# Two value chunks side by side at the start of a two-layer decoder trunk

## The chip, the cores and the metric

The kernel runs on one core of one Trainium2 chip. The metric is the device time of one execution in microseconds, the median of several runs. Beside the runs there is one profiled execution with its trace; times in it are counted from its first instruction.

## The reference

A decoder trunk of two layers over 256 positions of width 2048, in float32. Layer 1 is a block-sparse self-attention with 16 heads of 128 (with 256 positions there is a single block, so it is plain causal attention with a relative bias), layer 2 a sliding-window attention with shared keys and values. Each is followed by an output projection, a LayerNorm, a convolutional gated feed-forward part of width 5504 and a second LayerNorm. What the change touches is the start of layer 1:

```python
q, k, v = jnp.split(x @ w_qkv, 3, axis=-1)      # (256, 2048) @ (2048, 6144)
...
p = jax.nn.softmax(logits + bias)               # per head
out = p @ v
```

## The kernel before

All weights lie in one stream in memory, `wst`, cut into units of 128 x 1024 float32 (512 KB), in the order in which they are used. A unit is loaded into `raw` by SP (L103, four buffers). It is then split into a high part `wh` by ScalarE (L128) and a low remainder `wl` by VectorE (L157), with four buffers for these. TensorE multiplies high by high, high by low and low by high. The same split is made of x: `xc` is loaded (L220), ScalarE makes the high half of `xT` (L224), VectorE the low half (L225).

The order of work is written out by hand. `take()` hands out the next unit to TensorE; before that it queues the splits up to three units ahead (`AHEAD`), and after them whatever was left for this place with `at(n, ...)`, where n counts steps. `step()` is called after each unit and runs what was left with `pe_at`. So on ScalarE and VectorE, work that `at` left stands behind the split of the unit three ahead. The split of unit u needs the buffers of unit u - 4, which TensorE must have finished.

Layer 1 treats the 16 heads in four groups. `v_group()` computes 512 columns of the value projection (a chunk): x is stationary, weights move, and two accumulators of 128 x 512 take the two halves of the positions. A unit of weights holds two blocks of K (128 rows each) of one chunk, so a chunk is 8 units. `evac` copies the accumulators into `vt` (L751, ScalarE, placed with `at(0, ...)`). Then come, for each of the four heads, a query and a key unit pair (`feat_unit`, `ws_unit`: weights stationary, L300 and L303, two units each) and the steps of `attention`. The accumulators `acc` come from a pool of four, the tiles `at` from another of four.

The opening is written out in `load_input`: the first unit is loaded and split in two pieces of 512 columns, with one block of x behind each; then x (two blocks at a time) and units alternate. Between them `tables()` loads the small tables for the bias; a matmul (L275) after the fourth unit makes the bias rows. On POOL, `spread_bias` (L284, `ud` to `band`) and `load_bias` (L288, `band` to `bias`) run for each group of heads; each bias load waits for its band. `load_residual` (L246) loads x a second time, as the residual.

Of the kernel before, what the change touches and what calls it, by code (L numbers as in the profile page):

```python
# [18 lines left out]
P = 128  # L19
T = 256  # L20
D = 2048
KB = D // P
# [15 lines left out]
RAW_BUFS = 4  # L38
HALF_BUFS = 4
AHEAD = HALF_BUFS - 1  # L40
HW = 1024
# [36 lines left out]
def trunk(ctx: ExitStack, tc: tile.TileContext, wst, xT_in, x_in, relb, onehot, umask, sinks, conv_in, ln_g, ln_b, out):  # L78
# [14 lines left out]
    reach, placed = {}, {}  # L93

    def pieces(u):
        return (slice(0, HW // 2), slice(HW // 2, HW)) if u == 0 else (slice(0, HW),)

    def load_weights(behind=None):
        u = todo["load"]
        if u < n_halves:  # L100
            raws[u] = wpool.tile([P, HW], F32, name="raw")
            for j, c in enumerate(pieces(u)):
                nc.sync.dma_start(raws[u][:, c], wst[u][:, c])  # L103
                if behind:
                    behind(j)
            todo["load"] += 1
# [43 lines left out]
    def quad_low(s):  # L150
        q, (wh, wl) = quad[s], placed[s]
        minus(q.bl, q.shape(raws[s][:, 512:]), q.bh.bitcast(F32))
        minus(wl, q.tm[:, 0:HW], wh.bitcast(F32))

    def low_piece(s, c):
        wh, wl = placed[s]
        nc.vector.tensor_tensor(out=wl[:, c], in0=raws[s][:, c], in1=wh[:, c].bitcast(F32), op=ALU.subtract)  # L157

    def split_upto(i, behind=None):
        while todo["low"] <= min(i, n_halves - 1):  # L160
            s = todo["low"]
            high_upto(s, behind)
            if s in quad:
                quad_low(s)
                raws.pop(s - 1)
                load_weights()
            elif len(pieces(s)) == 1:
                if s - 1 in quad:
                    q = quad[s - 1]
                    nc.scalar.activation(q.uh, q.tm[:, 512:], AF.Copy)  # L170
                low_piece(s, slice(0, HW))
                if s - 1 in quad:
                    minus(q.ul, q.tm[:, 512:], q.uh.bitcast(F32))
            placed.pop(s)
            todo["low"] += 1
            if s + 1 not in quad:
                raws.pop(s)
                load_weights()
# [4 lines left out]
    def at(n, f, *a, first=False):  # L183

        fs = before.setdefault(slot["now"] + n, [])
        fs.insert(0 if first else len(fs), (f, a))
# [25 lines left out]
    xT = big.tile([P, KB, 2 * T], F32R, name="xT")  # L212
# [3 lines left out]
    def load_input(pool, tables):  # L216
        xc = pool.tile([P, KB, T], F32, name="xc", bufs=1)

        def load_x(k, n=2):
            (nc.scalar if n == 1 else nc.sync).dma_start(xc[:, k:k + n], xT_in[:, k:k + n, :])  # L220

        def split_x(k, n=2):
            ks = slice(k, k + n)
            nc.scalar.activation(xT[:, ks, 0:T], xc[:, ks], AF.Copy)  # L224
            nc.vector.tensor_tensor(out=xT[:, ks, T:2 * T], in0=xc[:, ks], in1=xT[:, ks, 0:T].bitcast(F32),  # L225
                                    op=ALU.subtract)

        load_weights(lambda j: load_x(j, 1))
        for c in range(1, RAW_BUFS):
            load_x(2 * c)  # L230
            load_weights()
        tables()
        load_x(2 * RAW_BUFS)
        split_upto(0, lambda j: split_x(j, 1))
        for c in range(1, KB // 2):
            if c + RAW_BUFS < KB // 2:
                load_x(2 * (c + RAW_BUFS))
            if c < HALF_BUFS:
                split_x(2 * c)
                split_upto(c)  # L240
            else:
                at(c - HALF_BUFS, split_x, 2 * c)

    def load_residual():
        for t in range(2):
# [145 lines left out]
    def acc_tile():  # L391
        return psum.tile([P, 512], F32, name="acc")
# [310 lines left out]
    def layer_attention(l, rest, stage, turnover):  # L703
        oT = st
        kept = []
        if l:
            norm, turned = rest
            turn, low = turned
            n0 = nexth["i"]
            c = COLS[1]  # L710
            norm(c[0])
            norm(c[1])
            split_upto(n0 + 7)
            norm(c[2])

            def early(t, i):
                if t == 0 and i == 5:
                    pts = [turn(c[j]) for j in range(2)]
                    low(c[0], pts[0])
                    norm(c[3])  # L720
                    low(c[1], pts[1])
                if t == 0 and i == 7:
                    low(c[2], turn(c[2]))
                if t == 1 and i == 1:
                    low(c[3], turn(c[3]))
                if t == 1 and i < HALF_BUFS:
                    split_upto(n0 + 8 + i)

            kept = [acc_tile(), acc_tile()]
            Moving(lambda k: xT[:, k, :], KB).chunk(kept, early=early)  # L730
        pool = stage(f"att{l}")
        bias = pool.tile([P, NH, 2 * P], F32, name="bias", bufs=1)
        if l == 0:
            load_input(pool, lambda: bias_table(pool))
        else:
            nc.vector.tensor_scalar(nsk, sk, -1.0, None, op0=ALU.mult)
        for i, h in enumerate(range(0, NH, 4)):
            n = (4 + 8 * i, 4 * i)[l]
            if l == 0:
                at(n, spread_bias, l, h, h + 4)  # L740
            at(n, load_bias, bias, l, h, h + 4)

        def v_group(accs=None):
            if not accs:
                accs = [acc_tile(), acc_tile()]
                Moving(lambda k: xT[:, k, :], KB).chunk(accs)
            vt = pool.tile([P, 2, 512], F32, name="vt", bufs=1 if l else 2)

            def evac():
                for t in range(2):  # L750
                    nc.scalar.activation(vt[:, t, :], accs[t], AF.Copy)  # L751

            at(0, evac)
            return vt

        def feat_unit(name, bufs):
            acc = acc_tile()
            ws_unit(acc)
            o = pool.tile([P, T], F32, name=name, bufs=bufs)

            def evac():
                nc.scalar.activation(o, acc[:, T:2 * T], AF.Copy)
                nc.vector.tensor_tensor(out=o, in0=acc[:, 0:T], in1=o, op=ALU.add)

            at(0, evac, first=True)
            return o

        if l == 0:
            for g in range(NH // 4):
                vt = v_group()  # L770
                for j in range(4):
                    h = 4 * g + j
                    q = feat_unit("qT", 4)
                    k = feat_unit("kT", 4)
                    attention(pool, l, h, q, vt[:, :, j * P:(j + 1) * P], k, bias, oT)
        else:
            vt = v_group(kept)
            ks = [feat_unit("kT", KVH) for _ in range(KVH)]
            for h in range(NH):
                q = feat_unit("qT", 4)  # L780
                j = h // GRP
                attention(pool, l, h, q, vt[:, :, j * P:(j + 1) * P], ks[j], bias, oT)
        return project_out(lambda k: oT[:, k, :], NH, 2 * l, turnover.homes, AF.Gelu_apprx_tanh, turnover)
# [130 lines left out]
def _moving(w):  # L914

    k, n = w.shape
    b = w.reshape(k // P, P, n // 512, 512).transpose(2, 0, 1, 3).reshape(-1, 2, P, 512)
    return b.transpose(0, 2, 1, 3).reshape(-1, P, HW)


def _paired(w):

    b = w.reshape(FT, P, NCH // 2, 2, 512).transpose(2, 0, 3, 1, 4)
    seq = np.stack([b[n, k, c] for n in range(NCH // 2) for k, c in paired_order(LEAD[n], GROUPS[n])[0]])
    return seq.reshape(-1, 2, P, 512).transpose(0, 2, 1, 3).reshape(-1, P, HW)


def _stream(w_qkv, w_o0, w_kv, w_q, w_o1, w_up, w_down):
    parts = []
    q, k, v = (w_qkv[:, i * D:(i + 1) * D] for i in range(3))  # L930
    for g in range(4):
        c = slice(512 * g, 512 * (g + 1))
        parts.append(_moving(v[:, c]))
        parts.append(np.stack([_still(q[:, c]), _still(k[:, c])], 1).reshape(-1, P, HW))

    def ffn(l):
        up = w_up[l]
        parts.append(np.stack([_still(up[:, :DFF]), _still(up[:, DFF:])], 1).reshape(-1, P, HW))
        parts.append(_paired(w_down[l]))

    parts.append(_moving(w_o0))
    ffn(0)
    parts.append(_moving(w_kv[:, 512:]))
    parts.append(_still(w_kv[:, :512]).reshape(-1, P, HW))
    parts.append(_still(w_q).reshape(-1, P, HW))
    parts.append(_moving(w_o1))
    ffn(1)
    return np.concatenate(parts, 0)
# [36 lines left out]
```

## Time and profile before

| | |
|---|---|
| median of 3 runs | 2074.72 us (2074.56 to 2074.79) |
| profiled execution, its own time | 2074.71 us |
| its span, first to last instruction | 2072.7 us |
| mean granted TensorE clock | 0.998 |
| TensorE, VectorE, ScalarE busy | 99%, 76%, 50% |
| memory read | 401.02 MB |

In a timeline row stand the start, the duration, the engine, the line, the operation with its output and inputs, and the idle time of the engine ahead of it with what ended it. PE is TensorE, DVE VectorE, ACT ScalarE, POOL GpSimd. Matmuls overlap: their durations are longer than the distance from one start to the next, so lost time on TensorE is read from starts. In a row of waits stand the total, the number and the longest. In a row of groups stand the total and the mean (in ns) of one.

### The profile page before, as it was taken

How to read it: one execution, taken by the hardware profiler on the slowest of the kernel's cores; microseconds unless marked ns; L12 is line 12 of the kernel's file. 1: busy time of each engine (PE TensorE's matmuls, PEld its weight loads, DVE VectorE, ACT ScalarE, POOL GpSimd, SP SyncE). 2: the span in 40 equal slices, each digit the busy share in tenths (PEclk: the TensorE clock that was granted, in tenths of full speed). 3: DMA queues.
4: the chain of work that ended last, by engine and by line, in shares of the span. 5: the costliest groups of instructions: out<-in, count | busy, mean ns of one | idle time of the engine just before them, and what ended most of it. 6: DMA issues, size and time to landing. Idle time of an engine off the chain costs nothing.

```text
span 2072.7 us, 28857 instructions
## 1 busy us (share of the span) xinstructions
PE 2058.5 (99%) x11004; PEld 1779.1 (86%) x11004; DVE 1575.2 (76%) x2310; ACT 1031.2 (50%) x1453; POOL 23.3 (1%) x36
## 2 busy tenths in 40 slices
PE   9999999999999999999999999999999999999997
PEld 7888888988888888888888888898888888888886
DVE  5555556787877877898986676788787787788886
ACT  5444444444545555454553555445545454555452
POOL 0100000000000000000000000000000000000000
PEclk9999999999999999999999999999999999999999
DMA  8855558455555555566685545736555555566563
GB/s 282 294 190 180 166 169 274 138 186 192 190 187 191 186 192 185 188 239 202 203 260 193 176 144 169 239 114 197 190 191 184 193 187 189 188 217 214 192 215 131
DMA packets 114266, 405.10 MB, mean 195 GB/s; under 512 B 15648, under 2 KB 15968, under 8 KB 112848
## 3 DMA queue, kind: packets, MB, share of 16 engines
q1 hardware_dynamic: 106832, 383.67, 56.4%
q0 software_dynamic: 7008, 19.33, 2.6%
q8 instruction: 86, 1.41, 0.3%
q14 instruction: 52, 0.43, 0.1%
q10 hardware_dynamic: 288, 0.26, 0.0%
HBM read 401.02 MB, written 6.34 MB: 197 GB/s over the span
## 4 chain that ended last, share of the span: by engine, by line
PE 99%; DVE 0%; DMA 0%; ACT 0%; SPq 0%; issue 0%
PE acc L300 38%; PE acc L303 20%; PE acc L483 6%; PE acc L484 6%; PE acc L485 6%; PE acc L353 5%; PE acc L354 5%; PE acc L355 5%; PE acc L318 1%; PE at L483 1%; PE at L484 1%; PE at L485 1%; PE acc L330 1%; PE at L653 1%; PE at L686 1%; PE at L679 1%
## 5 line engine op out<-in xcount | busy, mean ns | idle before, releaser
L157 DVE TENSOR_TENSOR wl<-raw,wh 128x1024 fp32r<-128x1024 f32 (+1 forms) x639 | 778.4, 1221 | 402.0 <-ACT wh L128 393.4
L128 ACT ACTIVATE wh<-raw 128x1024 fp32r<-128x1024 f32 (+1 forms) x639 | 674.8, 1058 | 685.4 <-issue 249.1
L300 PE MATMUL acc<-xT,wh 128*128 128x512 f32 x3456 | 872.3, 394 | 0.0
L300 PEld LDWEIGHTS acc<-xT,wh 128*128 128x128 f32 x3456 | 623.6, 189 | 112.9
L303 PEld LDWEIGHTS acc<-xT,wl 128*128 128x128 f32 x3456 | 471.4, 190 | 33.8
L303 PE MATMUL acc<-xT,wl 128*128 128x256 f32 x3456 | 481.8, 282 | 0.0
L484 PE MATMUL acc<-wl,up 128*128 128x512 f32 x360 | 140.1, 389 | 0.0
L483 PE MATMUL acc<-wh,up 128*128 128x512 f32 x360 | 140.1, 389 | 0.0
L485 PE MATMUL acc<-wh,up 128*128 128x512 f32 x360 | 140.1, 389 | 0.0
L839 DVE SCALAR_TENSOR_TENSOR work<-work,cw 128x255 f32<-128x255 f32 x172 | 83.2, 484 | 6.1
L840 DVE SCALAR_TENSOR_TENSOR work<-work,cw 128x254 f32<-128x254 f32 x172 | 83.1, 483 | 6.1
L485 PEld LDWEIGHTS acc<-wh,up 128*128 128x128 f32 x360 | 67.6, 188 | 14.1
L483 PEld LDWEIGHTS acc<-wh,up 128*128 128x128 f32 x360 | 67.6, 188 | 14.0
L484 PEld LDWEIGHTS acc<-wl,up 128*128 128x128 f32 x360 | 67.6, 188 | 13.9
L838 DVE TENSOR_SCALAR work<-work,cw 128x256 f32<-128x256 f32 x172 | 70.9, 412 | 6.2
L837 DVE TENSOR_TENSOR work<-acc,work 128x256 f32<-128x256 f32 x172 | 71.7, 417 | 1.5 <-ACT work L836 1.5
L836 ACT ACTIVATE work<-acc 128x256 f32<-128x256 f32 x172 | 62.8, 365 | 6.5 <-PE acc L330 6.5
L353 PE MATMUL acc<-wh,xT 128*128 128x512 f32 x144 | 58.7, 407 | 0.3 <-ACT wh L128 0.3
L354 PE MATMUL acc<-wl,xT 128*128 128x512 f32 x144 | 56.7, 393 | 0.8 <-DVE wl L157 0.8
L355 PE MATMUL acc<-wh,xT 128*128 128x512 f32 x144 | 56.5, 392 | 0.0
L195 ACT ACTIVATE work<-work 128x256 f32<-128x256 f32 x86 | 36.1, 420 | 38.6 <-DVE work L840 38.5
L147 ACT ACTIVATE wh<-work 128x1024 fp32r<-128x1024 f32 x24 | 25.5, 1063 | 47.0 <-DVE work L136 47.0
(197 smaller groups left out, 2210.0 us busy)
## 6 DMA issues: line engine op xcount, KB each, us to landing
raw<-in_wst_dram SPq DMA_DIRECT2D x723, 512.0 KB, 3.4
band<-ud POOLq DMA_DIRECT2D x8, 512.0 KB, 14.6
bias<-band POOLq DMA_DIRECT2D x8, 512.0 KB, 7.3
gb<-in_ln_g_dram POOLq DMA_DIRECT2D x4, 1024.0 KB, 6.3
gb<-in_ln_b_dram POOLq DMA_DIRECT2D x4, 1024.0 KB, 8.1
res<-in_x_dram POOLq DMA_DIRECT2D x2, 1024.0 KB, 7.5
out_dram<-res SPq DMA_DIRECT2D x8, 256.0 KB, 2.5
xc<-in_xT_dram SPq DMA_DIRECT2D x7, 256.0 KB, 5.7
```

What stands on the lines that cost most here:

```text
L128: nc.scalar.activation(wh[:, c], raws[s][:, c], AF.Copy)
L157: nc.vector.tensor_tensor(out=wl[:, c], in0=raws[s][:, c], in1=wh[:, c].bitcast(F32), op=ALU.subtract)
L300: nc.tensor.matmul(acc, cols(wh, j), xT[:, k, :], start=(k == 0), stop=False)
L303: nc.tensor.matmul(o, cols(wl, j), xT[:, k, 0:T], start=False, stop=(k == KB - 1))
L353: nc.tensor.matmul(acc, sh, wh, start=(k == 0), stop=False)
L354: nc.tensor.matmul(acc, sh, wl, start=False, stop=False)
L355: nc.tensor.matmul(acc, sl, wh, start=False, stop=(k == self.nk - 1))
L483: nc.tensor.matmul(acc, a[0], wh, start=key not in begun, stop=False)
L484: nc.tensor.matmul(acc, a[0], wl, start=False, stop=False)
L485: nc.tensor.matmul(acc, a[1], wh, start=False, stop=stop)
L839: nc.vector.scalar_tensor_tensor(c[:, 1:T], h[:, 0:T - 1], w[:, 1:2], c[:, 1:T], op0=ALU.mult, op1=ALU.add)
L840: nc.vector.scalar_tensor_tensor(c[:, 2:T], h[:, 0:T - 2], w[:, 0:1], c[:, 2:T], op0=ALU.mult, op1=ALU.add)
```

## The change

The value projections of the first two groups of heads are computed together, ahead of both groups. A unit of weights now holds one block of K for both chunks (`_moving_two`), the two chunks use four accumulators, and the 16 units run in the order block, chunk, half of the positions (`v_two_groups`). All four copies to `vt` are then placed at once. Chunks 2 and 3 stay as they are. The second unit of weights, like the first, is loaded and split in two pieces. The opening is ordered anew: both units in pieces first, with x in single blocks behind the first unit's pieces, then x, two units, x, the tables, x; the later loads and splits of x are placed by units. The bias loads are placed at other steps.

```diff
     def pieces(u):
-        return (...) if u == 0 else (slice(0, HW),)
+        return (...) if u < 2 else (slice(0, HW),)
...
         load_weights(lambda j: load_x(j, 1))
-        for c in range(1, RAW_BUFS):
-            load_x(2 * c)
-            load_weights()
+        load_weights()
+        load_x(2)
+        load_weights()
+        load_weights()
+        load_x(4)
         tables()
-        load_x(2 * RAW_BUFS)
+        load_x(6)
         split_upto(0, lambda j: split_x(j, 1))
-        for c in range(1, KB // 2):
-            if c + RAW_BUFS < KB // 2:
-                load_x(2 * (c + RAW_BUFS))
-            if c < HALF_BUFS:
-                split_x(2 * c)
-                split_upto(c)
-            else:
-                at(c - HALF_BUFS, split_x, 2 * c)
+        split_upto(1)
+        split_x(2)
+        for k in range(4, KB, 2):
+            if k > 6:
+                at(k - 7, load_x, k)
+            at(k - 3, split_x, k)
...
         for i, h in enumerate(range(0, NH, 4)):
-            n = (4 + 8 * i, 4 * i)[l]
+            n = (10 + 14 * i, 4 * i)[l]
...
+        def v_two_groups():
+            accs = [[acc_tile(), acc_tile()] for c in range(2)]
+            mv = Moving(lambda k: xT[:, k, :], KB)
+            for k in range(KB):
+                for c in range(2):
+                    wh, wl = mv.block()
+                    for t in range(2):
+                        mv.mm(accs[c][t], k, t, wh, wl)
+                step()
+            return [v_evac(a) for a in accs]
...
         if l == 0:
+            vts = v_two_groups()
             for g in range(NH // 4):
-                vt = v_group()
+                vt = vts[g] if g < 2 else v_group()
...
+def _moving_two(w):
+    return w.reshape(-1, P, HW)
...
     for g in range(4):
         c = slice(512 * g, 512 * (g + 1))
-        parts.append(_moving(v[:, c]))
+        if g == 0:
+            parts.append(_moving_two(v[:, 0:1024]))
+        if g > 1:
+            parts.append(_moving(v[:, c]))
```

More of the change, by code (lines that the diff above doesn't have):

```diff
@@ L95, in pieces @@
     def pieces(u):
-        return (slice(0, HW // 2), slice(HW // 2, HW)) if u == 0 else (slice(0, HW),)
+        return (slice(0, HW // 2), slice(HW // 2, HW)) if u < 2 else (slice(0, HW),)
     def load_weights(behind=None):
@@ L746, in v_group, with v_evac @@
                 Moving(lambda k: xT[:, k, :], KB).chunk(accs)
+            return v_evac(accs)
+        def v_two_groups():
[8 more added lines that the diff above has]
+            return [v_evac(a) for a in accs]
+        def v_evac(accs):
             vt = pool.tile([P, 2, 512], F32, name="vt", bufs=1 if l else 2)
```

## The prediction

> **What bounds the kernel now.** I read the page first, then the waits of TensorE, then the opening in order of time, because the diff touches only layer 1's value projection and what is loaded ahead of it. The page's busy times, its chain, and TensorE's waits over the whole span:
>
> ```profile
> span 2072.7 us, 28857 instructions
> ...
> PE 2058.5 (99%) x11004; PEld 1779.1 (86%) x11004; DVE 1575.2 (76%) x2310; ACT 1031.2 (50%) x1453; POOL 23.3 (1%) x36
> ...
> PE 99%; DVE 0%; DMA 0%; ACT 0%; SPq 0%; issue 0%
> ...
> PE at L254 <- POOL ident masks.py:199: 1.4, 1, 1.4
> PE acc L354 <- DVE wl L157: 0.8, 1, 0.8
> PE acc L353 <- ACT wh L128: 0.3, 1, 0.3
> ```
>
> TensorE carries 99% of the chain. It waits three times: for the identity matrix before the warm-up, which the change leaves alone, and twice for the second unit of weights. The diff keeps every matmul (it reorders them and adds none), so it can change the time only by the idle time of TensorE. What there is to win is a part of two waits; everything else it touches can only cost. The waits are listed by modelled matmul ends, so I measure them by starts. TensorE's timeline:
>
> ```profile
> 7.43 0.39 PE L355 MATMUL acc<-wh,xT 128*128 128x512 f32 x1
> ...
> 8.82 0.39 PE L355 MATMUL acc<-wh,xT 128*128 128x512 f32 x1
> 9.49 0.50 PE L353 MATMUL acc<-wh,xT 128*128 128x512 f32 x1 [0.28 <-ACT wh L128]
> 10.75 0.51 PE L354 MATMUL acc<-wl,xT 128*128 128x512 f32 x1 [0.76 <-DVE wl L157]
> 11.09 0.39 PE L355 MATMUL acc<-wh,xT 128*128 128x512 f32 x1
> ...
> 27.70 0.39 PE L355 MATMUL acc<-wh,xT 128*128 128x512 f32 x1
> ...
> 30.42 0.39 PE L355 MATMUL acc<-wh,xT 128*128 128x512 f32 x1
> ```
>
> Between the last two rows lie twelve steps, one unit of weights: 2.72 us, 0.227 us from start to start. After the matmul at 8.82 three more should start at 9.05, 9.28 and 9.50; the third starts at 11.09. So the opening loses 1.59 us, and that is the most the change can win there.
>
> **The opening.** Before, one unit of 512 KB holds two blocks of K for one chunk, so each 2.72 us of matmuls need 512 KB of weights and 256 KB of x. After, a unit holds one block of K for two chunks: 512 KB and 128 KB. The loads are reordered with it, and unit 1 comes in two pieces of 256 KB. ScalarE's timeline shows when the loads land, since each of these rows waited for one:
>
> ```profile
> 5.50 0.63 ACT L128 ACTIVATE wh<-raw 128x512 fp32r<-128x512 f32 x1 [0.38 <-DMA raw<-in_wst_dram]
> ...
> 7.17 0.63 ACT L224 ACTIVATE xT<-xc 128x512 fp32r<-128x512 f32 x1 [0.73 <-DMA xc<-in_xT_dram]
> 8.38 1.06 ACT L128 ACTIVATE wh<-raw 128x1024 fp32r<-128x1024 f32 x1 [0.58 <-DMA raw<-in_wst_dram]
> ...
> 10.32 1.06 ACT L128 ACTIVATE wh<-raw 128x1024 fp32r<-128x1024 f32 x1 [0.36 <-DMA raw<-in_wst_dram]
> ...
> 12.72 1.06 ACT L128 ACTIVATE wh<-raw 128x1024 fp32r<-128x1024 f32 x1 [0.82 <-DMA raw<-in_wst_dram]
> 14.91 1.06 ACT L128 ACTIVATE wh<-raw 128x1024 fp32r<-128x1024 f32 x1 [0.61 <-DMA raw<-in_wst_dram]
> ```
>
> By the order of issue these rows have 768, 1024, 1536, 2304, 3072 and 3840 KB behind them. I read the new order off that curve by its bytes, as estimates: the first piece of unit 1 (1024 KB) at 7.17, the second (1280) halfway to 8.38, at 7.78, x blocks 2 and 3 (1536) at 8.38, unit 2 (2048) at 9.67, unit 3 (2560) at 11.12, unit 4 (3584) at 14.18.
>
> Unit 0's twelve matmuls start as before and end at 9.05: its weights and x blocks 0 and 1 are still issued first. A piece costs one high and one low split:
>
> ```profile
> L157 DVE TENSOR_TENSOR wl<-raw,wh 128x1024 fp32r<-128x1024 f32 x33 | 40.2, 1223 | 31.9 <-ACT wh L128 31.8
> L157 DVE TENSOR_TENSOR wl<-raw,wh 128x512 fp32r<-128x512 f32 x2 | 1.4, 692 | 4.3 <-ACT wh L128 4.3
> L225 DVE TENSOR_TENSOR xT<-xc,xT 128x512 fp32r<-128x512 f32 x7 | 4.8, 687 | 0.6 <-ACT xT L224 0.6
> ```
>
> ScalarE then does unit 1's pieces from 7.17 and 7.80 (0.63 each), x 2 and 3 from 8.43, unit 2 from 9.67 to 10.73. VectorE does the low halves by 8.5 and 9.2, x by 9.84, and unit 2 from 10.76 to 11.99. TensorE asks for unit 1's first piece at 9.05 and 9.28, for its second at 10.41, and for unit 2 at 11.77 (high) and 12.00 (low). All are there, unit 2 with 0.01 us to spare. Unit 3 is asked for at 14.5 and split by 13.4; unit 4 is asked for at about 18.0, behind the bias table's two matmuls, and split by 16.6. The additional instructions (one issue on SP, one split on ScalarE, one on VectorE) lie inside these waits for loads. So the opening wins 1.59 us; as unit 2 has no margin and the curve is read between rows, I allow 0.6 us of new wait: the gain is between 1.0 and 1.6, and I take 1.59. The other x splits and the loads of x move one unit or more later, but a block is now used up in 2.72 us instead of 1.36, and each is still split three units ahead of its use.
>
> **What the change adds: the end of the two chunks.** There are four accumulators of this pool. Before, a chunk holds two, and the first query unit takes a third at once. After, the two chunks hold all four, and the first query unit takes the first again: it cannot start before ScalarE has copied that one out. That copy is put on ScalarE's queue behind the high split of the unit three ahead, and this split waits for the buffers of the very last unit of the chunks. The same order is in the trace at the end of chunk 0, where nothing on TensorE waits for it. Timeline, and the copy by shape:
>
> ```profile
> 30.65 1.98 PE L300 MATMUL acc<-xT,wh 128*128 128x512 f32 x8
> 30.84 1.06 ACT L128 ACTIVATE wh<-raw 128x1024 fp32r<-128x1024 f32 x1 [1.66 <-PE acc L355]
> 31.81 1.06 ACT L751 ACTIVATE vt<-acc 128x512 f32<-128x512 f32 x2
> 31.94 1.22 DVE L157 TENSOR_TENSOR wl<-raw,wh 128x1024 fp32r<-128x1024 f32 x1 [1.50 <-ACT wh L128]
> ...
> L751 ACT ACTIVATE vt<-acc 128x512 f32<-128x512 f32 x2 | 1.1, 582 | 0.0
> ```
>
> The last matmul starts at 30.42, the split at 30.84, the copies at 31.81, the first of them is done 0.58 later, at 32.39. TensorE follows ScalarE by 0.05 us (the split of 8.38 ends at 9.44, its matmul starts at 9.49). So the query matmul that started at 30.65 would start at 32.44: 1.79 us. The first step after such a gap was 0.34 instead of 0.23 (10.75 to 11.09), which adds 0.11: 1.90 us. Bounds: zero if the copy came out ahead of the split, 2.4 if the second copy were waited for too (0.48 more). I take 1.90, since the queue's order in the changed kernel is this one. The first accumulator is complete nine matmuls, 2.04 us, before the chunks' end, so the wait is one of queue order alone. Behind it, the key unit's accumulator is copied 0.48 us after the first and asked for 5 us later; the other two copies and the next split lie within the first query half. Nothing further is late.
>
> **What moves at no cost.** Only one handover from attention to a value chunk goes (chunk 1's own); TensorE waited at none of them, so this is worth nothing. The bias loads are queued on POOL at other places. POOL does not wait for TensorE's place in the program, only for its own transfers, so what counts is the order in its queue: the two residual loads now stand after the first bias load instead of after the third.
>
> ```profile
> 42.30 0.79 POOL L288 DMA_DIRECT2D bias<-band  x1 [13.73 <-DMA band<-ud]
> ...
> 73.09 0.78 POOL L288 DMA_DIRECT2D bias<-band  x1 [15.71 <-DMA band<-ud]
> 73.87 1.10 POOL L246 DMA_DIRECT2D res<-in_x_dram  x2
> 74.92 1.16 POOL L284 DMA_DIRECT2D band<-ud  x1
> ...
> raw<-in_wst_dram SPq DMA_DIRECT2D x723, 512.0 KB, 3.4
> ...
> raw<-in_wst_dram SPq DMA_DIRECT2D x6, 512.0 KB, 7.3
> res<-in_x_dram POOLq DMA_DIRECT2D x2, 1024.0 KB, 7.5
> band<-ud POOLq DMA_DIRECT2D x1, 512.0 KB, 17.7
> ```
>
> (The row with x723 is the page's, the last three are the DMA view of 74 to 92 us; the last column is the time to landing.) So the residual and one band run together at about 43 us instead of 74 us. At 74 us weights then took 7.3 us to land and TensorE never waited. The first bias is needed eight units (21.8 us) later than before and comes no later, so that gets looser. Cost: none, unless the cover is gone, which is the last rival.
>
> **Sum.** 0.31 us are added (1.90 less 1.59). The profiled execution took 2074.71 us, 2.0 more than its span of 2072.7, and the median of the runs is 2074.72, so the same sum holds for both: 2075.0 us. About 0.2%, 4.1 us, is what a measurement of this kernel can tell from no change; this is a thirteenth of it.
>
> **Rivals.** *The opening is not cured.* If unit 2 lands later than the curve says, its low split makes TensorE wait again, by at most the 1.59 that was lost before: 1.90 more, 2076.6 at worst. For it: 0.01 us of margin. Against: less data is ahead of it, and up to 10.32 the curve rises without a break. *The copy comes free.* If TensorE did not wait at the end of the chunks, the gain stays alone: 2073.1. For it: the accumulator is complete 2.04 us early. Against: the order on ScalarE shown above.
>
> *The clock falls back.* The warm-up rows show the clock at work: the first matmul pitch is 0.42 us, and only from the one at 7.43 on it is 0.23.
>
> ```profile
> 1.37 4.10 PE L254 MATMUL at<-ident 128*128 128x128 f32 x18 [1.37 <-POOL ident masks.py:199]
> ...
> 5.77 0.63 PE L354 MATMUL acc<-wl,xT 128*128 128x512 f32 x1
> 6.19 0.63 PE L355 MATMUL acc<-wh,xT 128*128 128x512 f32 x1
> ```
>
> The slow stretch is 6.06 us, from 1.37 to 7.43. If the new gap brought it back, half of such a stretch, 3.0 us, would be added: 2078.0. Against: after the gap of 1.59 us the matmul at 11.09 took 0.39 again. The Trainium skill's page TensorE: Matmul & The Clock Gate, section "A second HAM failure mode: psum-queue depth-cycling", says that short idle times between groups that cycle through accumulators made the clock fall back, which speaks against holding all four; its table in Part 1 asks for an idle window of about 3.4 us. By the first the time would be the 2078.0 of this rival, by the second the 2075.0 above.
>
> *Slower: weights late beside the residual.* From 43 us on, residual and band could hold back the weights. A load goes out when the low split frees its buffer, at 33.16 for the split of 31.94, which is 2.74 after the start of unit 7's last matmul, and is the load of unit 15. Unit 15 is asked for 0.23 + 7 x 2.72 = 19.27 after that start, less 1.2 for its split: the load has 15.4 us. Were it held for the whole of residual and band, 7.5 + 17.7 = 25.2 us, TensorE would wait 9.8 us: 2084.8. It decides from a landing time of 15.4 us, and passes 0.2% from about 19.3. For it: the x loads now reach further into this time. Against: 7.3 in the same company. The Trainium skill's page DMA: Bandwidth & Descriptors, section "Issuing engines are not separate DMA queues", says that transfers of all issuing engines interleave on the same 16; the 7.3 us, beside 3.4 over the whole kernel, agree with sharing, not with standing behind.
>
> **How the numbers follow.** Forecast 0.70 (2074.9 to 2075.6), opening not cured 0.12 (to 2076.6), copy free 0.09 (2073.1), clock 0.04, late weights 0.05. The range 2073.1 to 2076.8 takes in the first three. Only late weights pass 4.1 us upward: slower 0.04, and no case wins 4.1 us: faster 0.02 for what I do not see; same 0.94.
>
> **What would show it.** Right: no gap over 0.5 us in TensorE's starts between 7.4 and 17; one of about 2.0 us from start to start at about 50 us, ahead of the first query unit, put down to ScalarE's copy; matmuls of 0.39 behind it. Wrong: a wait for unit 2's low split near 12 us, no gap at the first query unit, steps of 0.42 after it, or waits for weights between 45 and 75 us. Any change beyond 0.31 that lies behind 60 us would be a cause that I have not named.

## The result and the profile after

| | before | after |
|---|---|---|
| median of 22 runs | 2074.6 us (2074.25 to 2076.39) | 2077.74 us (2075.72 to 2079.73) |
| profiled execution | 2074.71 us | 2078.07 us |
| its span | 2072.7 us | 2076.2 us |

The ratio is 1.0014 (95% interval 1.0008 to 1.002): slower by 3.1 us, beyond the interval and above the forecast range of 2073.1 to 2076.8. It is below the 0.2% named in the prediction, but the trace shows where nearly all of it is. The changed kernel also scatters over 4 us from run to run, where the kernel before mostly stays within 0.5.

TensorE's waits in the changed kernel (total, number, longest, us), and its timeline:

```profile
PE acc L300 <- ACT vt L766: 2.9, 1, 2.9
PE at L254 <- POOL ident masks.py:199: 1.4, 1, 1.4
PE acc L354 <- DVE wl L157: 0.5, 1, 0.5
PE acc L353 <- ACT xT L224: 0.2, 1, 0.2
```

```profile
6.41 0.40 PE L353 MATMUL acc<-wh,xT 128*128 128x512 f32 x1
...
11.21 0.39 PE L353 MATMUL acc<-wh,xT 128*128 128x512 f32 x1
12.14 0.50 PE L354 MATMUL acc<-wl,xT 128*128 128x512 f32 x1 [0.54 <-DVE wl L157]
12.48 0.40 PE L355 MATMUL acc<-wh,xT 128*128 128x512 f32 x1
...
50.87 0.39 PE L355 MATMUL acc<-wh,xT 128*128 128x512 f32 x1
54.20 2.50 PE L300 MATMUL acc<-xT,wh 128*128 128x512 f32 x8 [2.95 <-ACT vt L766]
56.50 1.91 PE L303 MATMUL acc<-xT,wl 128*128 128x256 f32 x8
58.21 0.63 PE L300 MATMUL acc<-xT,wh 128*128 128x512 f32 x1
```

The new gap is there, at the place that was named, but it is 3.33 us from start to start (50.87 to 54.20) instead of about 2.0. Behind it the eight matmuls of 256 columns (L303) span 1.91 us, where they spanned 1.12 in the kernel before:

```profile
32.46 1.12 PE L303 MATMUL acc<-xT,wl 128*128 128x256 f32 x8
```

The granted clock is the share of its full speed that TensorE was given, 1.00 being all of it. In the changed kernel it was (in each row, behind the two ends of a stretch: us, then each engine's busy time and instruction count, then the clock, the DMA share and GB/s):

```profile
50.00:55.00 5.00, 2.05 (x9) 1.39 (x8) 2.12 (x2) 2.39 (x4) 0.00 (x0) 1.00 1.03 380
55.00:59.00 4.00, 4.00 (x16) 3.55 (x15) 0.50 (x1) 1.67 (x3) 0.00 (x0) 0.59 0.73 236
59.00:70.00 11.00, 11.00 (x65) 9.67 (x64) 5.08 (x6) 4.66 (x6) 1.90 (x2) 0.99 0.75 212
...
54.20:55.74 1.54, 1.54 (x7) 1.28 (x8) 0.72 (x1) 1.41 (x3) 0.00 (x0) 1.00 0.81 314
55.74:59.15 3.41, 3.41 (x14) 3.03 (x13) 0.65 (x1) 1.06 (x1) 0.00 (x0) 0.50 0.74 231
```

The clock fell back to half for 3.41 us, from 55.74 to 59.15 (0.59 in the mean from 55 to 59). It did so 1.54 us after the gap had ended: the first seven matmuls behind the gap still ran at full clock. What made the gap longer stands in ScalarE's timeline:

```profile
48.57 1.06 ACT L128 ACTIVATE wh<-raw 128x1024 fp32r<-128x1024 f32 x1 [1.66 <-PE acc L355]
52.61 1.06 ACT L128 ACTIVATE wh<-raw 128x1024 fp32r<-128x1024 f32 x1 [2.97 <-DMA raw<-in_wst_dram]
53.57 2.04 ACT L766 ACTIVATE vt<-acc 128x512 f32<-128x512 f32 x4
```

The split of unit 19 waited for its weights, not for its buffer. By the prediction's own offsets it would have started at 51.29 (0.42 behind the matmul at 50.87); it started at 52.61, 1.32 us later, and the copy behind it was as late. POOL's timeline, and the DMA view of 42 to 56 us (the last column is the time to landing):

```profile
40.76 1.10 POOL L246 DMA_DIRECT2D res<-in_x_dram  x2
41.81 1.15 POOL L284 DMA_DIRECT2D band<-ud  x1
63.59 0.79 POOL L288 DMA_DIRECT2D bias<-band  x1 [20.63 <-DMA band<-ud]
...
raw<-in_wst_dram SPq DMA_DIRECT2D x5, 512.0 KB, 9.3
band<-ud POOLq DMA_DIRECT2D x1, 512.0 KB, 21.5
```

The account, from starts: before, the first 96 steps of the value projection end with the matmul at 30.42, and 96 more would put the last one at 52.18; after, it is at 50.87, so the opening wins 1.31. The gap costs 3.33 less 0.23, or 3.10, the slow first step behind it 0.10, the half-speed stretch 1.57 (the sum of each start-to-start distance above its usual one). The handover from attention to chunk 1, which the change removes, wins about 0.27: with the gap and the late weights out of the way (the run with both edits below), the first two groups of heads and chunk 2 take 124.41 us from the first query start, from 51.21 to 175.62; before, the same matmuls and chunk 1's 96 steps (21.76 us) take 146.43, from 30.65 to 177.08. The sum is 3.19. From 197 us to the end every matmul starts 3.25 us later than before; the profiled executions differ by 3.36.

### The profile page after: what moved, and what is told of

It reads as the page before. It is cut to its first block, busy times and chain, and to the rows that moved or that the text cites. A ratio compares the mean times of both kernels' runs of the same rounds, so it can differ in the third digit from the quotient of the medians.

```text
span 2076.2 us, 28867 instructions
## 1 busy us (share of the span) xinstructions
PE 2059.1 (99%) x11004; PEld 1779.2 (86%) x11004; DVE 1576.2 (76%) x2311; ACT 1031.7 (50%) x1454; POOL 23.3 (1%) x36
## 4 chain that ended last, share of the span: by engine, by line
PE 98%; DMA 1%; DVE 0%; ACT 0%; SPq 0%; issue 0%; ACTq 0%
PE acc L300 38%; PE acc L303 20%; PE acc L483 6%; PE acc L484 6%; PE acc L485 5%; PE acc L353 5%; PE acc L354 5%; PE acc L355 5%; PE acc L318 1%; PE at L483 1%; PE at L484 1%; PE at L485 1%; DMA raw<-in_wst_dram 1%; PE acc L330 1%; PE at L653 1%; PE at L686 1%
## 5 line engine op out<-in xcount | busy, mean ns | idle before, releaser
L303 PEld LDWEIGHTS acc<-xT,wl 128*128 128x128 f32 x3456 | 472.2, 191 | 34.0
L303 PE MATMUL acc<-xT,wl 128*128 128x256 f32 x3456 | 482.6, 283 | 0.0
```

Of the source, the lines that this page charges most:

```text
L303: nc.tensor.matmul(o, cols(wl, j), xT[:, k, 0:T], start=False, stop=(k == KB - 1))
```

## The experiments

Theory A: the gap is 2.0 us of queue order plus 1.3 us of late weights, these are late because the residual loads were brought forward, and the clock fell back because the gap became long. Each run's own times of the kernel before have medians of 2074.9 to 2075.1, since some of its executions (11 of 33 in the first set of runs) take about 1.7 us more, at a mean granted clock of 0.997 instead of 0.998. No trace is of one of these, so their cause is not shown. Differences under 0.5 us are not read. The interval of each ratio is about 1.9 us wide to either side: by time alone, only the runs whose interval leaves out 1 differ from the kernel before, and the rest is read from the traces.

**Residual back behind the third bias load**

```diff
-    at(24, load_residual)
+    at(39, load_residual)
```

> The changed kernel with the residual loads put behind the third bias load on POOL's queue, where they stood before; nothing else. Theory A: the gap of 3.33 us ahead of the first query unit is 2.0 us of queue order on ScalarE plus 1.3 us by which the weights of unit 19 came late because the residual ran beside them; the clock fell back because the gap passed 3 us. Then the gap is 2.0 us from start to start, the steps behind it are 0.23 us, and the time is 2075.0 (1.3 and about 1.5 less than the changed kernel's 2077.7). Theory B: the residual has no part in it (the band and the x loads made the weights late): the gap stays at 3.3, the time at 2077.7. Theory C: the gap shrinks but the clock falls back after any gap of 2 us: 2076.4.

2075.2 us (2074.8 to 2075.45, 11 runs), ratio 1.0 (0.999 to 1.0009). ScalarE, TensorE, and the DMA view of 42 to 56 us:

```profile
51.46 1.06 ACT L128 ACTIVATE wh<-raw 128x1024 fp32r<-128x1024 f32 x1 [1.66 <-PE acc L355]
52.42 2.04 ACT L766 ACTIVATE vt<-acc 128x512 f32<-128x512 f32 x4
```

```profile
51.03 0.39 PE L355 MATMUL acc<-wh,xT 128*128 128x512 f32 x1
53.05 2.14 PE L300 MATMUL acc<-xT,wh 128*128 128x512 f32 x8 [1.63 <-ACT vt L766]
55.03 1.10 PE L303 MATMUL acc<-xT,wl 128*128 128x256 f32 x8
```

```profile
raw<-in_wst_dram SPq DMA_DIRECT2D x5, 512.0 KB, 7.0
```

The split waits for TensorE's buffer again, the gap is 2.02 us, the eight matmuls span 1.10. Weights land in 7.0 instead of 9.3 us in the median; the load of unit 19 itself, issued at 42.93 here and at 42.76 in the changed kernel, takes 7.1 instead of 9.7. Theory A as to both parts; B and C fall. The scatter of 4 us goes with it.

**Copies ahead of the split of unit 19**

```diff
-            return [v_evac(a) for a in accs]
+            return [v_evac(a, True) for a in accs]
...
-        def v_evac(accs):
+        def v_evac(accs, now=False):
...
-            at(0, evac)
+            evac() if now else at(0, evac)
```

> The changed kernel with the four copies of the value accumulators put on ScalarE's queue ahead of the split of unit 19; the residual stays early. Theory A: the first copy runs while TensorE still works on chunk 1, TensorE does not wait at the first query unit whatever the weights do (unit 19 is asked for three units later), the clock stays: 2077.7 less 3.1 less 1.5, about 2073.2, which is 1.4 below the kernel before. Theory B (weights late for TensorE itself): a gap of over 1 us moves to unit 19, at about 59 us, and the time is above 2074.5.

2074.03 us (2073.3 to 2074.95, 11 runs), ratio 0.9995 (0.9986 to 1.0003). The residual is still early, and ScalarE still waits for weights; TensorE does not notice:

```profile
50.95 0.39 PE L355 MATMUL acc<-wh,xT 128*128 128x512 f32 x1
51.17 1.98 PE L300 MATMUL acc<-xT,wh 128*128 128x512 f32 x8
```

```profile
52.24 1.06 ACT L128 ACTIVATE wh<-raw 128x1024 fp32r<-128x1024 f32 x1 [0.27 <-DMA raw<-in_wst_dram]
54.80 1.06 ACT L128 ACTIVATE wh<-raw 128x1024 fp32r<-128x1024 f32 x1 [1.49 <-DMA raw<-in_wst_dram]
```

So the late weights cost only through what stands behind them on ScalarE.

**Both edits**

> Both edits: copies ahead of the split, residual behind the third bias load. Theory A: with the copies first the residual's place no longer matters, so the same as with the copies alone, about 2073.2. Theory B: the residual also costs elsewhere (weights waited for between 43 and 60 us): faster than the copies alone by over 0.5 us.

2073.31 us (2073.05 to 2074.12, 11 runs), ratio 0.999 (0.9981 to 0.9998). This is 0.7 us less than with the copies alone, which by its number is theory B. The profiled executions of the two are equal (2073.3 and 2073.31), with no gap between 13 and 60 us in either, so where the other executions lose it is not shown.

**The kernel before, with the residual early**

```diff
-    at(24, load_residual)
+    at(5, load_residual)
```

> The kernel before with one part of the change alone: the residual loads behind the first bias load. Theory A: TensorE has no place near 45 us where it waits on ScalarE's queue, so later weights are hidden by the units split ahead: within 0.3 us of the kernel before, no new gap. Theory B: late weights stop TensorE by themselves: a gap of 1 us or more between 45 and 60 us, and 2075.7 or more.

2074.7 us (2074.53 to 2076.67, 11 runs), ratio 1.0 (0.9991 to 1.0009). There is no new gap, though the band there took 19.2 us to land from 42 to 56 us. As theory A has it: by itself the move is free. The test is milder than the changed kernel, as weights landed in 6.9 us in that stretch (5.5 in the kernel before), not in 9.3.

**A longer gap with no transfer touched: one, two and four more copies**

```diff
-                for t in range(2):
+                for t in ((0,) * 1 + (0, 1) if l == 0 and slot['now'] <= 16 else range(2)):
                     nc.scalar.activation(vt[:, t, :], accs[t], AF.Copy)
```

These have the residual late, and `* 1`, `* 2` or `* 4`.

> The changed kernel with the residual late and the first accumulator of each of the two chunks copied twice. A copy added 0.63 us to the gap before (3.28 us with two more, 4.54 with four more), so the gap is 2.65 us. Theory A (an activity window that runs free of the program decides, so that a gap near its length is caught in some executions only: none at 2.02, eight of eleven at 3.28, all at 4.54): a few executions fall back, most are at 2075.2 + 0.63 = 2075.8. Theory B (a sharp limit just below 3.3 us): all executions within 0.4 us of 2075.8.

> The changed kernel with the residual late (its gap was 2.02 us, from start to start, and the clock held) and the first accumulator of each of the two chunks copied three times instead of once, which keeps the first query unit waiting for two more copies of 0.48 us. No transfer is touched. Theory A (the clock falls back by the length of the gap, somewhere above 2 us): the gap is 2.98 us; steps of 0.43 us behind it if the limit lies below 3 us, and then about 2075.2 + 0.96 + 1.4 = 2077.6, or 2076.2 with the clock held. Theory B (what threw the clock back was the busy DMA engines or the late weights, not the gap): steps of 0.23 us and 2076.2.

> The same with five copies instead of one: the gap is 3.94 us, longer than the changed kernel's 3.33, with the residual still late. Theory A: the clock falls back and stays at half speed for some 3 us as it did behind 3.33 us: 2075.2 + 1.92 + 1.4 = 2078.5. Theory B: the clock holds, 2077.1.

| more copies | gap, start to start | time, 11 runs | with the clock held it would be | ratio |
|---|---|---|---|---|
| 0 | 2.02 us | 2075.2 (2074.8 to 2075.45) | 2075.2 | 1.0 (0.999 to 1.0009) |
| 1 | 2.65 us | 2077.03 (2075.63 to 2077.79) | 2075.8 | 1.0005 (0.9996 to 1.0014) |
| 2 | 3.28 us | 2077.92 (2076.57 to 2079.97) | 2076.5 | 1.0013 (1.0004 to 1.0022) |
| 4 | 4.54 us | 2079.64 (2078.91 to 2080.55) | 2077.7 | 1.0021 (1.0012 to 1.0029) |

A copy more cost 0.63 us, not 0.48, presumably because each writes what the last one wrote; so the fourth column is 2075.2 plus the longer gap. With one more, five executions lie between 2075.6 and 2076.2 and six between 2077.0 and 2077.8; with two more, three lie between 2076.5 and 2076.8 and eight from 2077.7 on. The profiled ones with one and two more are of the lower group, and hold the clock; the one with four more fell back. The windows of 55 to 59 us, with two more and with four more copies:

```profile
55.00:59.00 4.00, 4.00 (x23) 3.44 (x22) 1.01 (x1) 2.89 (x5) 1.90 (x2) 1.00 0.68 178
```

```profile
55.00:59.00 4.00, 3.44 (x9) 2.71 (x10) 0.00 (x0) 3.87 (x8) 1.90 (x2) 0.61 0.82 240
```

The gap's length makes the clock fall back, with neither the residual nor late weights near it. There is no sharp limit in the length alone: none of the executions at 2.02 us is that slow, some are at 2.65 and 3.28, and all are at 4.54. That the upper groups at 2.65 and 3.28 are the clock is inferred: no trace is of one. For it speak their distance (about 1.5 us; the half-speed stretch of the changed kernel cost 1.57 in the trace) and the mean granted clock on record, which is 0.998 in all eight executions of the lower groups and 0.997 or less in ten of the fourteen of the upper ones. The kernel before has two groups too, but the run with the residual late has the opening of these three and shows one group, all eleven at 0.998.

**Both edits, and the third unit of weights in two pieces**

```diff
-        return (...) if u < 2 else (slice(0, HW),)
+        return (...) if u < 3 else (slice(0, HW),)
```

> Copies first, residual late, and the third unit of weights in two pieces as well. Left over in the opening is the wait for unit 2's low split (1.26 us from start to start where 0.23 is the step, with copies first and residual late). If that wait is the split of a whole unit standing behind one landing, as its 1.06 and 1.22 us suggest, halves of 0.63 and 0.69 are ready 1 us earlier: the wait goes or falls below 0.3 us, 2072.4. If it is the landing itself that is late, the wait moves to the second piece and the time stays at 2073.3.

2072.18 us (2072.14 to 2072.87, 11 runs), ratio 0.9986 (0.9978 to 0.9995): the fastest here, 2.8 us below the kernel before. TensorE waits for the identity matrix alone:

```profile
PE at L254 <- POOL ident masks.py:199: 1.4, 1, 1.4
```

The low split of unit 2 started at 10.98 with both edits and starts at 9.52 with a third unit in pieces. About 0.5 us of this is earlier landing in that execution (the split of x ahead of it starts at 8.09 instead of 8.58), the rest the pieces. What was late was the split of a whole unit, not the landing.

**The parts of the opening: pieces alone, layout alone**

The condition in `pieces` alone is changed: in the kernel before, and in the version with both edits.

```diff
-if u == 0 else      # kernel before: two kernels
+if u < 2 else       # second unit in pieces
+if u < 3 else       # second and third unit in pieces
...
-if u < 2 else       # both edits
+if u == 0 else      # second unit whole again
```

> The kernel before with one part of the change alone: the second unit of weights in two pieces, its order of loads and its chunks untouched. Theory A (the opening's gain comes from the pieces: the first low split is ready sooner): the two waits of 0.44 and 1.03 us near 9.5 us shrink to under 0.4 together, 2073.5. Theory B (it comes from the halved need of x for each unit, with two chunks side by side): less than 0.5 us gained, 2074.2 or more.

2073.85 us (2073.58 to 2074.88, 11 runs), ratio 0.9994 (0.9985 to 1.0003). Part of either theory: the wait at unit 1 shrinks (0.41 above the step), and one of 0.70 appears at the next whole unit.

> The kernel before, chunks one after the other, with the second and the third unit of weights in two pieces. Theory A (whole-unit splits are all that TensorE waits for in the opening): the two waits left with two units in pieces (0.41 and 0.70 us from start to start above the step) fall below 0.3 together, and the time is 2072.9, near the 2072.2 of the best version. Theory B (the need of 256 KB of x for each unit is what is late): the wait at the third unit stays at over 0.5 us and the time at 2073.5 or more.

2073.31 us (2073.0 to 2074.43, 11 runs), ratio 0.9991 (0.9982 to 1.0): between the theories. Without any change of layout the pieces bring 1.7 of the 2.8 us that the fastest version gains. Above the step, 0.24 us are left at the second unit's high split and 0.50 at its low split, though that unit is in pieces, and 0.19 at the fourth unit, which is whole.

> Copies first, residual late, chunks side by side, but the second unit of weights in one piece again. Theory A (the pieces make the opening's gain): the low split of unit 1 is ready 0.6 us later and unit 2's split behind it too: 1.0 us above the version with pieces, 2074.3. Theory B (the layout makes it): within 0.4 us of 2073.3.

2072.84 us (2072.7 to 2073.59, 11 runs), ratio 0.9989 (0.998 to 0.9998). Theory A missed: without the pieces it is no slower, and 0.47 us faster, just outside theory B's 0.4. A row of TensorE's timeline with both edits, then a row of its waits with unit 1 whole:

```profile
12.26 0.50 PE L354 MATMUL acc<-wl,xT 128*128 128x512 f32 x1 [0.76 <-DVE wl L157]
```

```profile
PE acc L354 <- DVE wl L157: 0.5, 2, 0.3
```

One wait of 1.03 us above the step at unit 2, or two of 0.45 and 0.43 at units 1 and 2: both come to unit 2's low split, which starts on VectorE at 10.98 and at 10.95. With chunks side by side the pieces of unit 1 move the wait and do not remove it; the pieces of unit 2 do.

## Why the prediction was wrong

**What bounds the kernel** was right in the main: idle time of TensorE moved the time, nearly all of it ahead of 60 us. The clock moved it too, which this part left out. And the handover that goes was put at nothing because TensorE did not wait there, but was worth about 0.27 us.

**The opening** was right in its sum, 1.31 against 1.59 taken and 1.0 to 1.6 allowed. What set it was the low split of unit 2, ready at 12.08 (started at 10.86, 1.22 long) where 11.99 was forecast: TensorE took up the matmul that needs it at 12.14 instead of 12.00, and the slow step behind it cost 0.11 more. TensorE had come there sooner than forecast, with steps of 0.23 us from 6.41 instead of 7.43, and waited from 11.21 to 12.14: the lead was lost there.

**The gap's queue order** was right: 2.02 us with the residual late, 2.0 forecast, and no gap with the copies first.

**The step that failed is "Cost: none" for the residual's move.** The prediction asked when unit 19's weights must be there for TensorE, and found 15.4 us. But the change itself had put the copy that TensorE waits for behind the split of that unit, so the deadline that counted was the split's. By the same arithmetic, a load is issued 2.74 us after the start of one unit's last matmul, and the split that needs it comes up four units later: 4 x 2.72 + 0.42 - 2.74 = 8.6 us, not 15.4. The load of unit 19 took 9.7 us, and the split was 1.32 us late. The landing time was the second part of the error: the 7.3 us taken from the stretch at 74 us would have met even 8.6. With the residual late the same load took 7.1, so the residual accounts for the difference; why it cost less at 74 us is not shown. So the missing 1.3 us is a wait that two parts of the change make together, each of which is free or cheaper without the other (residual alone: 2074.7; queue order alone: 2075.2).

**The clock rival** was priced for a gap of 1.9 us and given 0.04; it never came about at such a gap (none of 11 runs at 2.02). The two rivals, clock and late weights, were held apart, and it was the one that led to the other: late weights made the gap 3.33 and only then the clock fell. Its price, 3.0, was twice too high, as the measured stretch was 3.41 us long, not 6, and cost 1.57. What it was weighed against could not decide it: the 1.59 us are two waits, with idle times of 0.28 and 0.76 us, and a matmul at full speed right behind a gap proves nothing, since in the changed kernel seven of them came before the clock fell.

## What to carry to other kernels

When a change makes TensorE wait for a copy, everything ahead of that copy on its engine's queue becomes a deadline too: look there again for transfers that were hidden up to now, before calling a reordered transfer free. Price rivals in chains and not one by one: a gap of 2 us cost its own length here, while one of 3.33 cost 3.10 us and half as much again through the clock. In an opening, the split of a whole unit can be the wait; half units removed it with the chunks side by side, once they were carried to the last unit that is asked for early, and shortened it with the chunks one after the other.

## What the runs showed of the hardware

The clock of TensorE fell back to half behind one gap of 3.33 us from start to start, for 3.41 us. At 2.65 and 3.28 us the times fall in two groups, at 2.02 all stay low, at 4.54 all are high. The Trainium skill's page TensorE: Matmul & The Clock Gate, table of Part 1, has the clock fall after at least one idle window of about 3.4 us; the window is said there to run free of the kernel, which suits the two groups. The gap of 3.33, of which 2.95 were idle by the modelled ends of the matmuls, is shorter than such a window and fell back in the trace, so here the measurement sets the limit lower.

The traces allow an estimate of that limit. In the clock records of all thirteen, each stretch at full clock, from its rise to its next fall, is a whole multiple of 3.413 us (51.20 us is 15 of them, and 2058.24, in the kernel before, 603), as if the clock could change only at the ends of windows of that length; where these lie differs from execution to execution. The windows counted on from the rise of the clock, and the idle times by modelled ends, give the longest idle time within one window:

| gap, start to start | idle time of the gap | longest idle time within one window | clock in that trace |
|---|---|---|---|
| 2.02 us | 1.63 us | 1.63 us | held |
| 2.65 us | 2.26 us | 1.30 us | held |
| 3.28 us | 2.89 us | 1.76 us | held |
| 3.33 us (changed kernel) | 2.95 us | 1.87 us | fell at the end of that window |
| 4.54 us | 4.15 us | 3.06 us | fell at the end of that window |

So the estimate from these five is that about 1.8 of 3.41 us are enough. For a gap that starts anywhere in a window with equal chance, this gives 0, 7, 9 and 11 of 11 executions at 2.02, 2.65, 3.28 and 4.54 us; by their times it was 0, 6, 8 and 11. The limit rests on two traces that fell back, and no run tested it by itself.

The section on a second failure mode, which the prediction weighed, speaks of frequent short gaps; no run here has them.

With the residual's two transfers beside them, 512 KB loads of weights landed in 9.3 us in the median and the band in 21.5; with the residual late, from 42 to 56 us as well, in 7.0 and 15.0. This agrees with the interleaving that the Trainium skill's page DMA: Bandwidth & Descriptors, section "Issuing engines are not separate DMA queues", describes.
